# A two-block network on one core: down weights as whole images in the convolutions' buffers, modulation beside the up projection, sums of activations on VectorE alone

## The chip, the core and the metric

The kernel runs on one core of one Trainium2 chip. The metric is the device time of one execution in microseconds (us). The engines of the core work side by side, each through its own list of instructions in a fixed order: TensorE (PE, matmuls, whose weight loads stand as PEld), VectorE (DVE), ScalarE (ACT), GpSimd (POOL), and SyncE (SP), which issues the DMA transfers one behind the other. An instruction waits on semaphores until its inputs are written and its buffer is free, and everything behind it on its engine waits with it.

## The reference

Two blocks run one after the other on 1024 tokens of width 1024. The first has two layers, each an attention mixer and a gated MLP with a short convolution; the second is a recurrent and convolutional mixer whose norms are modulated by a condition vector. What the change touches is the MLP and the two preparations for the second block:

```python
def conv_gated_mlp(h, w_up, conv_w, conv_b, w_down):     # d_ff 2816, so w_up has 5632 columns
    u = h @ w_up
    up = jnp.pad(u, ((0, 0), (half, half), (0, 0)))
    c = conv_b
    for i in range(CONV_W):                               # 3 taps over the tokens
        c = c + up[:, i:i + s] * conv_w[i]
    gate, val = jnp.split(c, 2, axis=-1)
    return (jax.nn.gelu(gate, approximate=True) * val) @ w_down
...
    mod = jax.nn.silu(c) @ mod_w[l] + mod_b[l]            # modulation: 1024 x 3072, two vectors
    mod_k = jax.nn.silu(c_ctx) @ mod_w[l] + mod_b[l]
    hk = rms_norm_2(ctx, norm_g[l]) * (1.0 + scale_k) + shift_k
    vk = jnp.einsum('btd,de->bte', hk, lp['w_in'][:, :BRANCH_W])
    _, state_k = rglru(vk, lp, h0)                        # context: 256 tokens, gives start states
```

All of it is float32. The kernel gets that precision from TensorE by splitting each operand into a rounded high part and a low remainder and adding three products (high by high, high by low, low by high).

## The kernel before

The activations stand with channels on the 128 partitions and tokens along a row, in two halves of 512 tokens (`hf` 0 and 1), so an "image" is one group of 128 output channels for one half of the tokens: a PSUM tile of 128 x 512. Each operand is split by `split` (line 236): a cast on ScalarE (L239) makes the high part, a subtraction on VectorE or GpSimd (L240) the low one. All matmuls of this program part carry line L233.

Buffers come from pools by tag, each with a fixed number of tiles: `wr` (3 tiles of 128 x 512, raw weights as they land), `wh` and `wl` (2 each of 128 x 1024, their split parts), `v` (4 of 128 x 1024, the convolutions' accumulators), `p` (5), `q` (10) of 128 x 1024, `cb` (3 of 128 x 512, copies of PSUM tiles, also used by the context work), `pj`, `pt`, `pf`, `x`. PSUM has the tags `A` (2 tiles of two banks), `T` (2), `O` and `J` (1 each). A scheduler sets the order on each engine from the program's order and the tiles' dependences. So a tile's tag decides whose release a transfer waits for.

`ffn` is one layer's MLP. It runs these stages:

- `up_first` computes the images 0 and 1 of the up projection (the gate and the value half each) directly; `sums` then builds the sums and differences of the activations that the next stage needs.
- `pair(j)` for j = 2 to 21 computes one gate image and one value image for both token halves with seven half-size products (84 matmuls of 512 columns) instead of eight. Weights come in two 512 KB transfers into `q`. The products are joined through copies of PSUM tiles (`kept`, ScalarE, L1075) and additions back into PSUM (`add`, VectorE, L1079); s1 is made on GpSimd, s2 (L1090) and a12 - s2 (L1095) on VectorE, a11 - a21 on GpSimd. Pairs alternate between the PSUM tags T, T, O, J and the two tiles of A. `convolve` (L988 on ScalarE, L993 on VectorE) and `gate` (GELU L1002 on ScalarE, product L1003 on VectorE) finish a pair and store it to `sc_g`.
- `phase(0)`, then `phase(1)`: the down projection for one token half. `down_first(hf)` makes images 0 and 1 and loads the gated activations (`load_g`) on its way; `down(hf, m)` makes images 2 to 7, each in three thirds of 24, 24 and 18 matmuls with 1024, 1024 and 768 weight columns. Every image ends with `put`, a copy out of PSUM on ScalarE (L1159). `finish(0)` (the norm behind the MLP and the next norm) runs inside the start of phase 1, `finish(1)` behind it.

`feed` is work of the second block, given out step by step between the program's own. In layer 0 it is `modulation`, 25 steps: one loads the condition into two `p` tiles, the other 24 each load two chunks of 256 KB (`modw`, L1272) into `wr` and multiply and add them up on VectorE in four operations of 128 x 512 (L1275), each with a read of its sum and a little arithmetic behind. In layer 1 it is `context`, with matmuls of its own and tiles in `cb` and `wr`. `down` takes `n_feed[hf]` steps behind each third: (1, 1) in layer 0, (2, 1) in layer 1.

## Time and profile before

| What | Value |
|---|---|
| median of 3 runs | 3916.99 us (3916.99 to 3918.07) |
| the profiled execution | 3918.27 us, span 3916.5 us |
| TensorE busy | 90% of the span |
| VectorE, ScalarE, GpSimd busy | 63%, 47%, 52% |

"Busy" is the time in which an engine executed something; TensorE can be busy and still run at half the clock, or lose small gaps between matmuls, so the share alone does not tell how far a stage is from its floor. For that one compares a stage's length with its number of matmuls.

| Stage (us from the start of the span) | layer 0 | layer 1 |
|---|---|---|
| `up_first`, `sums`, first pair | 735 to 880 | 2265 to 2400 |
| the other pairs | 880 to 1277 | 2400 to 2806 |
| phase 0, images 2 to 7 | 1277 to 1393 | 2806 to 2950 |
| phase 1, images 0 and 1, with `finish(0)` | 1393 to 1438 | 2950 to 2998 |
| phase 1, images 2 to 7 | 1438 to 1554 | 2998 to 3088 |

### The profile page before, as it was taken

What the parts mean: (1) busy time and instruction counts of PE and PEld (TensorE: products, weight loads), DVE (VectorE), ACT (ScalarE), POOL (GpSimd) and SP (SyncE); (2) the same over time, 40 slices, a digit from 0 to 9 for tenths busy, and PEclk for the clock granted to TensorE, in tenths of its full rate; (3) what the DMA queues carried; (4) which work ended last, traced back from release to release, by engine and by line L of the source; (5) the groups of instructions that cost most, each with busy time, mean ns of one, the idle gap of its engine ahead of it and who ended that gap; (6) DMA issues with size and microseconds to landing.
All of it is one profiled execution on the core that took longest, in us unless ns stands there. A gap on an engine that the chain in (4) does not pass through costs nothing. (4 is left out here: it accounts for less than half of the span.)

```text
span 3916.5 us, 47759 instructions
## 1 busy us (share of the span) xinstructions
PE 3507.2 (90%) x16588; PEld 2833.4 (72%) x16588; DVE 2466.0 (63%) x3384; ACT 1830.7 (47%) x3293; POOL 2028.5 (52%) x1520
## 2 busy tenths in 40 slices
PE   6999899879999878999889888999889989897998
PEld 4788678667777656778778757777767768776786
DVE  5566866776566572467785876656535287686547
ACT  4455755444445232355665544445574323324343
POOL 3445433676557454534543566656656454545444
PEclk9999999899999989999999989999989989998999
DMA  3633653422224453354363432221535211111114
GB/s 98 163 117 124 203 160 124 167 75 76 81 79 137 154 180 127 105 135 152 130 209 129 149 118 81 81 81 64 164 102 165 88 46 55 45 49 38 51 52 142
DMA packets 227841, 440.12 MB, mean 112 GB/s; under 512 B 29584, under 2 KB 56464, under 8 KB 227600
## 3 DMA queue, kind: packets, MB, share of 16 engines
q1 hardware_dynamic: 227600, 437.08, 35.2%
q8 instruction: 130, 2.13, 0.2%
q14 instruction: 111, 0.91, 0.1%
HBM read 313.75 MB, written 104.34 MB: 107 GB/s over the span
## 5 line engine op out<-in xcount | busy, mean ns | idle before, releaser
L240 POOL TENSOR_TENSOR wlZ<-wrZ,whZ 128x512 fp32r<-128x512 f32 (+1 forms) x484 | 665.6, 1391 | 738.1 <-ACT whZ L239 658.3
L233 PE MATMUL AZ<-xZ,whZ 128*128 128x512 f32 x2624 | 830.5, 398 | 75.9 <-ACT cbZ L1075 30.9
L233 PEld LDWEIGHTS AZ<-xZ,whZ 128*128 128x128 f32 x2624 | 497.6, 191 | 198.0 <-ACT cbZ L1075 39.4
L239 ACT CAST whZ<-wrZ 128x512 fp32r<-128x512 f32 (+1 forms) x484 | 277.1, 601 | 633.5 <-issue 163.6
L233 PE MATMUL AZ<-xZ,wlZ 128*128 128x512 f32 x1312 | 522.5, 398 | 19.4 <-POOL wlZ L240 18.8
L524 POOL TENSOR_TENSOR ptZ<-pfZ,ptZ 128x512 fp32r<-128x512 f32 (+1 forms) x200 | 262.6, 1313 | 362.3 <-DVE ptZ L523 330.5
L233 PE MATMUL JZ<-xZ,whZ 128*128 128x512 f32 (+1 forms) x1280 | 415.9, 402 | 35.0 <-DVE xZ L240 7.2
L240 POOL TENSOR_TENSOR wlZ<-qZ,whZ 128x512 fp32r<-128x512 f32 x200 | 264.7, 1340 | 159.6 <-ACT whZ L239 159.6
L522 ACT COPY pfZ<-TZ 128x512 f32<-128x512 f32 (+2 forms) x400 | 220.3, 556 | 206.2 <-PE TZ L517 128.3
L233 PEld LDWEIGHTS AZ<-xZ,wlZ 128*128 128x128 f32 x1312 | 250.8, 191 | 84.2 <-POOL wlZ L240 31.4
L233 PEld LDWEIGHTS JZ<-xZ,whZ 128*128 128x128 f32 (+1 forms) x1280 | 232.2, 187 | 93.6 <-DVE xZ L240 8.3
L233 PE MATMUL TZ<-xZ,whZ 128*128 128x512 f32 x864 | 274.8, 398 | 27.1 <-ACT cbZ L1075 13.2
L540 PE MATMUL OZ<-ptZ,vZ 128*128 128x256 f32 (+1 forms) x1344 | 260.6, 306 | 34.4 <-DVE ptZ L524 11.6
L523 DVE CAST ptZ<-pfZ 128x512 fp32r<-128x512 f32 (+2 forms) x400 | 222.7, 559 | 106.9 <-ACT pfZ L522 91.7
L517 PE MATMUL TZ<-ident,pZ 128*128 128x128 f32 x1488 | 243.4, 283 | 22.0 <-ACT pfZ L522 12.2
L233 PE MATMUL JZ<-xZ,wlZ 128*128 128x512 f32 (+1 forms) x640 | 253.6, 396 | 0.7 <-POOL wlZ L240 0.7
L540 PEld LDWEIGHTS OZ<-ptZ,vZ 128*128 128x128 f32 x1344 | 204.1, 196 | 60.8 <-DVE ptZ L524 17.3
L517 PEld LDWEIGHTS TZ<-ident,pZ 128*128 128x128 f32 x1488 | 181.2, 145 | 54.7 <-ACT pfZ L522 20.9
L239 ACT CAST whZ<-qZ 128x512 fp32r<-128x512 f32 x200 | 116.1, 618 | 213.6 <-issue 139.5
L233 PEld LDWEIGHTS TZ<-xZ,whZ 128*128 128x128 f32 x864 | 164.1, 191 | 68.3 <-ACT cbZ L1075 14.0
L233 PE MATMUL AZ<-qZ,whZ 128*128 128x512 f32 x544 | 179.9, 413 | 26.7 <-ACT pjZ L1159 13.4
L562 DVE TENSOR_REDUCE s1Z<-AZ 128x1 f32<-128x1024 f32 x128 | 155.9, 1221 | 66.2 <-PE AZ L233 35.1
(505 smaller groups left out, 7919.6 us busy)
## 6 DMA issues: line engine op xcount, KB each, us to landing
wrZ<-wdn SPq DMA_DIRECT2D x160, 256.0 KB, 2.8
qZ<-wup SPq DMA_DIRECT2D x80, 512.0 KB, 3.4
wrZ<-wi SPq DMA_DIRECT2D x156, 256.0 KB, 2.7
sc_g<-vZ SPq DMA_DIRECT2D x44, 512.0 KB, 3.4
qZ<-sc_pr SPq DMA_DIRECT2D x40, 512.0 KB, 4.8
wrZ<-wo SPq DMA_DIRECT2D x64, 256.0 KB, 2.9
sc_ot<-cbZ SPq DMA_DIRECT2D x56, 256.0 KB, 2.4
xZ<-sc_ot SPq DMA_DIRECT2D x56, 256.0 KB, 5.6
```

The costliest lines, as they stand in the source:

```text
L233: self.nc.tensor.matmul(ps, lhsT=a, rhs=b, start=first and k == 0, stop=last and k == n - 1, skip_group_check=parts)
L239: nc.scalar.copy(h, full)
L240: (eng or nc.vector).tensor_tensor(out=l, in0=full, in1=h.bitcast(F32), op=ALU.subtract)
L517: nc.tensor.transpose(ps[:, n:n + 128], blk, self.ident)
L522: nc.scalar.copy(pf[:, 0:n], ps[:, 0:n])
L523: nc.vector.tensor_copy(ph[:, 0:n], pf[:, 0:n])
L524: (nc.gpsimd if SHARE[self.turn2 % len(SHARE)] else nc.vector).tensor_tensor(out=pl[:, 0:n], in0=pf[:, 0:n], in1=ph[:, 0:n].bitcast(F32), ...
L540: nc.tensor.matmul(o[:, c0:c0 + w], lhsT=v, rhs=x[:, at[k]:at[k] + w], start=(k == order[0] and x is ph), stop=(k == order[-1] and x is pl ...
L562: nc.vector.tensor_reduce(out=nmx, in_=ps, axis=AX.X, op=ALU.max, negate=True)
```

## The change

Five edits go together.

1. `down` takes its weights through a new `w_tile`: one transfer of the whole third (512 or 384 KB) into a `v` tile, instead of two of 256 KB into `wr`. The split into `wh` and `wl` is still made in pieces of 512 columns, the low part on GpSimd. `down_first` keeps `wr`. `finish(0)` takes its scratch tiles from `cb` instead of `v`.
2. In layer 0 one step of the modulation is given out ahead of each of the 20 pairs; the five that are left go to `phase(0)`. In layer 1 six steps of the context are given out in `down_first(0)`. No steps are left for phase 1.
3. All subtractions and splits of `sums`, and the splits of `prenorm`, are on VectorE. Before, GpSimd had a quarter of the subtractions and half of the splits of `sums`, and every second split of the fast `prenorm`.
4. In `pair` the first copy (p1) goes to a `wr` tile instead of `cb`, and the two PSUM sets are swapped between even and odd pairs. `up_first` uses single banks O, T and J for image 0 and A for image 1, and gates image 1 first.
5. `down_first(0)` uses a tile of A instead of O and T.

```diff
 def finish(hf, pause=None):
-    return nxt(self.post(y[hf], ("ffn_post", l * 8), src, dst, hf, 7 * hf, pause), hf, pause)
+    tag = "v" if hf else "cb"
+    return nxt(self.post(y[hf], ("ffn_post", l * 8), src, dst, hf, 7 * hf, pause, tag), hf, pause, tag)
...
-            def sub(o, x, y, k):
-                (nc.gpsimd if k == 3 else nc.vector).tensor_tensor(out=o, in0=x, in1=y, op=ALU.subtract)
+            def sub(o, x, y):
+                nc.vector.tensor_tensor(out=o, in0=x, in1=y, op=ALU.subtract)
...
-                    self.split(t, h, lo, nc.gpsimd if k % 2 else nc.vector)
+                    self.split(t, h, lo, nc.vector)
...
-            self.split(t, h, l, nc.gpsimd if fast and c % 2 else nc.vector)
+            self.split(t, h, l)
...
-            def kept(ps):
-                t = self.t("cb")
+            def kept(ps, tag="cb"):
+                t = self.raw() if tag == "wr" else self.t(tag)
                 nc.scalar.copy(t, ps)
                 return t
...
-            if j % 2 == 0:
+            if j % 2:
                 c11, c12, c21, c22 = (self.ps(t) for t in "TTOJ")
...
-            p1 = kept(c22)
+            p1 = kept(c22, "wr")
...
-            a = [self.ps("A") for _ in range(2)]
+            a = [[self.ps("O"), None], [self.ps("T"), None]]
...
-            b = [[], []]
-            for v in range(2):
-                b[v].append(self.ps("T" if v else "O"))
-                self.proj(ws[v], xs, 0, b[v][0])
-            for v in range(2):
-                b[v].append(self.ps("T" if v else "J"))
-                self.proj(ws[v], xs, 1, b[v][1])
+            b = [halves(self.ps("A")) for _ in range(2)]
+            for hf in range(2):
+                for v in range(2):
+                    self.proj(ws[v], xs, hf, b[v][hf])
...
             for v in range(2):
+                a[v][1] = self.ps("JT"[v])
                 first(v, 1)
-            gate(0, [convolve(v * 22, [(a[v], 0, T)]) for v in range(2)])
             gate(1, cs)
+            gate(0, [convolve(v * 22, [(a[v][0], 0, 512), (a[v][1], 512, 512)]) for v in range(2)])
...
-            ps = halves(self.ps("A")) if hf else [self.ps("O"), self.ps("T")]
+            ps = halves(self.ps("A"))
...
+                if l and not hf:
+                    feed.step()
                 yield
...
+        def w_tile(src, n):
+
+            raw = self.t("v")
+            nc.sync.dma_start(raw[:, 0:n], src)
+            h, lo = (self.wp.tile([128, 1024], F32R, name=self.nm(t), tag=t, bufs=WB) for t in ("wh", "wl"))
+            for c in range(0, n, 512):
+                c = slice(c, min(n, c + 512))
+                self.split(raw[:, c], h[:, c], lo[:, c], nc.gpsimd)
+            return h, lo
...
-                w = self.weight(I["wdn"][l, m][:, k0 * 128:(k0 + n) * 128], n * 128)
+                w = w_tile(I["wdn"][l, m][:, k0 * 128:(k0 + n) * 128], n * 128)
...
         for j in range(2, 22):
+            if not l:
+                feed.step()
             pair(j, *ts)
-        n_feed = (2, 1) if l else (1, 1)
+        n_feed = (2, 0) if l else (1, 0)
```

Three places show what this does to the engines' lists. On SyncE, in phase 1 of layer 0, before (L208 loads down weights, L1272 the modulation's; the number behind a tag is the tile's):

```order
L1272 DMA wrZ2833_13063<-modw 128x512
L1272 DMA wrZ2836_13069<-modw 128x512
L208 DMA wrZ2841_13079<-wdn 128x512
L208 DMA wrZ2842_13083<-wdn 128x256
L1272 DMA wrZ2843_13105<-modw 128x512
L1272 DMA wrZ2846_13111<-modw 128x512
```

In the changed program SyncE's list has this in the same part of the program, at the end of phase 0 (L1180 is `w_tile`, L1151 is `load_g`):

```order
L1180 DMA vZ2733_12556<-wdn 128x1024
L1180 DMA vZ2736_12588<-wdn 128x768
L1180 DMA vZ2855_13063<-wdn 128x1024
L1180 DMA vZ2858_13095<-wdn 128x1024
L1151 DMA qZ2744_12632<-sc_g 128x512
L1180 DMA vZ2861_13127<-wdn 128x768
L1151 DMA qZ2745_12636<-sc_g 128x512
```

Down weights and modulation no longer alternate in one queue over the same three tiles; the weights of the first third of phase 1 now stand ahead of the loads of the gated activations.

On ScalarE, around the p1 copy of a pair in bank A, before:

```order
L988 ACTIVATE vZ2256_9799<-OZ2241_9668,pv_91 128x512
L239 CAST whZ2266_9868<-pZ2259_9811 128x512
L239 CAST whZ2266_9868<-qZ2257_9809 128x512
L1075 COPY cbZ2264_9835<-AZ2261_9815 128x512
L239 CAST whZ2269_9902<-qZ2258_9810 128x512 x2
L1075 COPY cbZ2265_9865<-AZ2260_9814 128x512
```

In the changed program:

```order
L989 ACTIVATE vZ2231_9441<-OZ2218_9312,pv_91 128x512
L1076 COPY wrZ2245_9491<-AZ2242_9471 128x512
L239 CAST whZ2250_9543<-qZ2238_9465 128x512
L239 CAST whZ2250_9543<-qZ2239_9466 128x512
L239 CAST whZ2253_9577<-qZ2239_9466 128x512
L239 CAST whZ2253_9577<-qZ2263_9625 128x512
L1076 COPY cbZ2248_9523<-AZ2241_9470 128x512
```

The p1 copy now stands ahead of the casts of the next weights; the second copy (p5) stands behind four casts, where it had two.

On VectorE, between a T, T, O, J pair and the next pair in bank A, before (L1003 is the gate's product, L1079 the addition of p1):

```order
L993 SCALAR_TENSOR_TENSOR vZ2218_9507<-OZ2203_9376,pv_91,vZ2218_9507 128x512
L993 SCALAR_TENSOR_TENSOR vZ2218_9507<-OZ2203_9376,pv_91,vZ2218_9507 128x511
L993 SCALAR_TENSOR_TENSOR vZ2218_9507<-JZ2204_9377,pv_91,vZ2218_9507 128x512
L1003 TENSOR_TENSOR vZ2217_9500<-vZ2217_9500,vZ2218_9507 128x1024
L1079 TENSOR_TENSOR AZ2222_9522<-AZ2222_9522,cbZ2226_9543 128x512
```

In the changed program (ISA L1287 are the modulation's operations, L1080 is the addition):

```order
L994 SCALAR_TENSOR_TENSOR vZ2181_9121<-OZ2168_8992,pv_91,vZ2181_9121 128x511
L994 SCALAR_TENSOR_TENSOR vZ2181_9121<-JZ2169_8993,pv_91,vZ2181_9121 128x512
L1287 ISA pZ2208_9293,mpZ2106_8650<-wrZ2207_9291,pZ2085_8500 128x512
L1287 ISA mpZ2106_8650 128x1
L1287 ISA pZ2209_9295,mpZ2106_8650<-wrZ2207_9291,pZ2086_8501 128x512
L1287 ISA mpZ2106_8650 128x1
L1080 TENSOR_TENSOR AZ2191_9150<-AZ2191_9150,wrZ2195_9171 128x512
L1004 TENSOR_TENSOR vZ2180_9114<-vZ2180_9114,vZ2181_9121 128x1024
```

Two of the modulation's four operations stand ahead of the addition of p1, and the gate's product now stands behind it.

## Rows read from the trace of the kernel before

**Rows 1.** Windows: length; busy us (xinstructions) of PE, PEld, DVE, ACT, POOL; PEclk; DMA

```profile
880.00:1277.00 397.00, 372.00 (x1603) 298.21 (x1602) 236.53 (x281) 197.93 (x325) 246.01 (x179) 1.00 0.27 93
1277.00:1393.00 116.00, 98.45 (x399) 73.98 (x398) 71.93 (x184) 33.38 (x59) 47.90 (x39) 0.99 0.56 174
1393.00:1438.00 45.00, 41.21 (x161) 31.67 (x161) 30.41 (x32) 19.48 (x35) 28.83 (x20) 0.92 0.62 196
1438.00:1554.00 116.00, 96.74 (x387) 75.09 (x385) 35.25 (x83) 31.89 (x58) 49.62 (x41) 0.90 0.40 125
2806.00:2950.00 144.00, 120.24 (x541) 96.97 (x539) 58.56 (x83) 97.81 (x171) 75.92 (x66) 0.91 0.39 116
2998.00:3088.00 90.00, 87.18 (x380) 70.88 (x379) 12.00 (x13) 30.46 (x56) 49.35 (x40) 1.00 0.39 117
```

**Rows 2.** Timeline, ScalarE: start, duration, line, operation; copies of the last two images

```profile
1537.65 0.58 ACT L1159 COPY pjZ<-OZ 128x512 f32<-128x512 f32 x1
...
1553.48 0.58 ACT L1159 COPY pjZ<-TZ 128x512 f32<-128x512 f32 x1
```

**Rows 3.** Waits of TensorE, 1277 to 1393: total us, times, longest

```profile
PE AZ L233 <- POOL wlZ L240: 7.3, 12, 1.2
```

**Rows 4.** Waits of TensorE, 1438 to 1554

```profile
PE AZ L233 <- ACT whZ L239: 11.7, 2, 10.1
PE AZ L233 <- ACT pjZ L1159: 5.4, 2, 4.8
```

**Rows 5.** The modulation's line: ns min/median/max, first and last start; its wait

```profile
L1275 DVE CUSTOM_DVE_ANT_0 pZ<-wrZ,pZ x96: 677/689/1769, 1280.0 to 1486.7; 128x512 f32<-128x512 f32 x96
...
  DMA wrZ<-modw: 58.2, 33
```

**Rows 6.** Timeline around 1454; in brackets the idle time before and its releaser

```profile
1453.51 0.62 ACT L239 CAST whZ<-wrZ 128x512 fp32r<-128x512 f32 x1 [6.41 <-DMA wrZ<-wdn]
...
1454.18 1.22 PE L233 MATMUL AZ<-xZ,whZ 128*128 128x512 f32 x2 [10.07 <-ACT whZ L239]
```

**Rows 7.** Waits of TensorE in layer 0's pairs, 880 to 1277

```profile
PE AZ L233 <- ACT cbZ L1075: 19.6, 16, 1.8
PE AZ L233 <- DVE AZ L1079: 2.8, 10, 0.4
```

**Rows 8.** The same in layer 1's pairs, 2400 to 2806

```profile
PE AZ L233 <- ACT cbZ L1075: 19.2, 15, 2.0
```

**Rows 9.** Timeline of one pair of layer 0 in bank A

```profile
1013.76 0.39 PE L233 MATMUL AZ<-xZ,wlZ 128*128 128x512 f32 x1
...
1018.52 0.39 PE L233 MATMUL AZ<-xZ,wlZ 128*128 128x512 f32 x1
...
1020.36 0.72 PE L233 MATMUL AZ<-qZ,whZ 128*128 128x512 f32 x2 [1.46 <-ACT cbZ L1075]
...
1028.19 0.73 PE L233 MATMUL AZ<-xZ,whZ 128*128 128x512 f32 x2 [1.53 <-ACT cbZ L1075]
```

**Rows 10.** Groups of VectorE in layer 0's pairs: busy us, mean ns, idle before

```profile
L993 DVE SCALAR_TENSOR_TENSOR vZ<-AZ,pv,vZ 128x512 f32<-128x512 f32 x37 | 27.7, 748 | 27.9 <-ACT vZ L988 27.6
...
L1079 DVE TENSOR_TENSOR AZ<-AZ,cbZ 128x512 f32<-128x512 f32 x36 | 24.9, 691 | 78.2 <-PE AZ L233 70.1 <-ACT whZ L239 8.1
L1095 DVE TENSOR_TENSOR qZ<-qZ,pZ 128x512 f32<-128x512 f32 x17 | 24.4, 1437 | 0.5 <-POOL wlZ L240 0.4
```

**Rows 11.** DMA issues of the page: KB each, median us to landing

```profile
wrZ<-wdn SPq DMA_DIRECT2D x160, 256.0 KB, 2.8
qZ<-wup SPq DMA_DIRECT2D x80, 512.0 KB, 3.4
```

**Rows 12.** Waits of TensorE, head of layer 0's up projection

```profile
PE TZ L233 <- ACT cbZ L1075: 6.6, 1, 6.6
```

**Rows 13.** Timeline, ScalarE, just before that wait

```profile
832.76 1.06 ACT L1002 ACTIVATE vZ<-vZ 128x1024 f32<-128x1024 f32 x1 [5.46 <-DVE vZ L993]
```

**Rows 14.** Waits of TensorE, layer 1's down projection, 2806 to 2950

```profile
PE TZ L233 <- ACT cbZ L239: 13.6, 3, 8.4
```

More of the change, by code (lines that the diff above doesn't have):

```diff
@@ L290, in mean_sq, with prenorm @@
         return ps
-    def prenorm(self, xn, gain, fast=False, keep=None, pause=None):
+    def prenorm(self, xn, gain, fast=False, keep=None, pause=None, tag="v"):
         nc = self.nc
-        R = self.rstd(self.mean_sq(xn, 1024, fast=fast, bank="T", pause=pause), self.eps, EPS, stay=True)
+        R = self.rstd(self.mean_sq(xn, 1024, tag, fast, "T", pause), self.eps, EPS, tag, stay=True)
         out = []
@@ L329, in load_x, with post @@
         return xn
-    def post(self, y, gain, src, dst, hf, fast=False, pause=None):
+    def post(self, y, gain, src, dst, hf, fast=False, pause=None, tag="v"):
         nc = self.nc
-        R = self.rstd(self.mean_sq(y, 1024, fast=fast, pause=pause), self.eps, EPS, stay=True)
+        R = self.rstd(self.mean_sq(y, 1024, tag, fast, pause=pause), self.eps, EPS, tag, stay=True)
         sl = slice(hf * 512, hf * 512 + 512)
@@ L1036, in sums @@
             for k in range(4):
[L1037 removed]
+                sub(b11[k], b12[k], b11[k])
             put(b11, one("pj"))
             for k in range(4):
[L1040 removed]
+                sub(b12[k], b22[k], b12[k])
             for k in range(4):
[L1042 removed]
+                sub(b22[k], b22[k], b11[k])
             put(b22, lambda k: halves(self.t("q", F32R)))
             for k in range(4):
[L1045 removed]
+                sub(b21[k], b21[k], b22[k])
             put(b12, lambda k: one("pt" if k < 3 else "pf")(k))
@@ L1122, in first @@
             def first(v, hf):
-                ps = a[v][:, hf * 512:hf * 512 + 512]
-                self.mm3(ps, [(tuple(p[:, c % 4 * 128:c % 4 * 128 + 128] for p in own[v][c // 4]), xs[hf][c]) for c in range(8)])
+                self.mm3(a[v][hf], [(tuple(p[:, c % 4 * 128:c % 4 * 128 + 128] for p in own[v][c // 4]), xs[hf][c]) for c in range(8)])
             for v in range(2):
@@ L1285, in modulation, with modnorm @@
                                            op0=ALU.add, op1=ALU.mult)
-    def modnorm(self, xn, which, fast=False, pause=None):
+    def modnorm(self, xn, which, fast=False, pause=None, tag="v"):
         nc = self.nc
-        R = self.rstd(self.mean_sq(xn, 1024, fast=fast, bank="T", pause=pause), self.eps, EPS, stay=True)
+        R = self.rstd(self.mean_sq(xn, 1024, tag, fast, "T", pause), self.eps, EPS, tag, stay=True)
         out = []
@@ L1784, in emit @@
                     feed.add(net.context())
-                    nxt = lambda xn, hf, pause: net.modnorm(xn, 0, fast=hf == 1, pause=pause)
+                    nxt = lambda xn, hf, *a: net.modnorm(xn, 0, hf == 1, *a)
                 xs = net.ffn(l, xs, cur, SC[p], nxt, feed)
```

6 lines of the change are left out of this document (1 added, 5 removed).

## The prediction

> **What bounds the kernel now.** TensorE does, nearly everywhere, so the question for each stage is how much of its time is more than its matmuls need. I first took the spacing of matmuls where nothing stalls: between the two low-part matmuls of [rows 9] at 1013.76 and 1018.52 lie 21 matmuls, so one costs 4.76 / 21 = 0.227 us. Then I read the windows by stage [rows 1] and multiplied the matmul counts by that. Phase 0 of layer 0 (second row): 399 x 0.227 = 91 of 116 us, 25 lost. Phase 1, images 2 to 7 (fourth row): 387 x 0.227 = 88 of 116, 28 lost, with the granted clock at 0.90 of the full 2.4 GHz, so part of the loss is spent in matmuls at the half level of 1.2 GHz. The same stage of layer 1 (last row), which runs beside no fed work: 380 x 0.227 = 86 of 90, 4 lost, clock 1.00. That stage is the control: it uses the old `wr` transfers too, so the loss in layer 0 is not in the down projection itself. Within layer 0 the last image has no modulation beside it, and it took 1553.48 - 1537.65 = 15.8 us [rows 2], where 66 matmuls need 15.0. The pairs of layer 0 (first row of [rows 1]): 1603 x 0.227 = 364 of 397, 33 lost.
>
> Then the waits. In phase 1 of layer 0 TensorE waits 11.7 us for casts of weights in two pieces, and 5.4 us for copies out of PSUM [rows 4]. The longest piece is seen in [rows 6]: TensorE stood 10.07 us for a cast, and ScalarE had itself stood 6.41 us for the transfer of those weights. VectorE stood 58.2 us, in 33 pieces, for the modulation's transfers [rows 5]. Both wait for the other in turn: three `wr` tiles, filled by one queue, hold both kinds, so a weight waits for a reduction and a reduction for a weight's split. In the pairs the waits are short and regular: 16 of about 1.2 us for `kept` copies in layer 0, 15 in layer 1 [rows 7, 8]; [rows 9] show the two of one pair in bank A, for p1 (1.46) and p5 (1.53).
>
> **The change part by part.**
>
> *Layer 0's down projection.* Weights leave `wr`, and 20 of 25 feed steps leave the stage; phase 1 keeps none. If phase 1 then runs like its control it loses 4 / 90 of its length, that is 5 of 116, and gains 28 - 5 = 23. Phase 0 keeps five steps (10 transfers, 20 reductions), in front of a weight queue that they no longer share tiles with; I take 6 lost and a gain of 25 - 6 = 19. The stage between (third row of [rows 1]: 161 x 0.227 = 37 of 45) has the norm inside and stays. Together -42. The upper end is all of both losses, -53; the lower end is what the named waits on weights and copies carry: 11.7 + 5.4 + 7.3 [rows 3, 4] = 24. The 7.3 us for low parts on GpSimd may stay, since `w_tile` splits there too. I take -42, nearer to the control.
>
> Whole images: a third now lands with one 512 KB transfer. By [rows 11] 256 KB took 2.8 us and 512 KB 3.4, so the first half comes 0.6 us later and the second earlier than two in a row; with four `v` tiles the loads stand up to a stage ahead, and I cost this at nothing. Should that lead be lost, it is 0.6 us a third, 18 thirds a phase, 11 us a phase.
>
> *The modulation in layer 0's pairs.* 19 of the 24 groups of reductions move there (the step that loads the condition takes one of the 20 places): four reductions of 0.689 us (median; 0.677 to 1.769, [rows 5]) and about 0.5 of small ones. At the median this is 4 x 0.69 + 0.5 = 3.3 us a pair, at the longest 4 x 1.77 + 0.5 = 7.6. VectorE has 236.5 / 19 = 12.4 us of work in a pair of 397 / 19 = 20.9 us [rows 1], so it goes to 15.7 or, at the worst, 20.0. The reduction's nearest rows are in the same stage: an operation with one operand in SBUF takes 748 ns there, one with two takes 1437 [rows 10]. A reduction has two, so I take 1.44: 4 x 1.44 + 0.5 = 6.3, and 18.7 of 20.9. That fits, but what matters is who is queued behind. In bank A two reductions stand ahead of the addition of p1: 2 x 1.44 + 0.2 = 3.1 us, where the gate's product (about as long as two operations, 1.4 to 2.9) stood before. The next matmuls into that tile come nine matmuls after the p1 product's last, 9 x 0.227 = 2.0 us, and waited 2.8 us in all before [rows 7]. So I add 0.5 us to each of ten such pairs, +5. The other subtractions (s2, a12 - s2) are listed tens of matmuls ahead of their use and are covered. SyncE gets two more transfers a pair behind q2; their tiles come free by reductions of the pair before, so the next q1 waits for no new engine.
>
> The Trainium skill, page "SBUF — State Buffer", section "Who interferes with whom", says that a VectorE instruction with two SBUF inputs and a GpSimd instruction that reads SBUF exclude each other, whichever issued first. The two means in [rows 10] agree with that; by that rule GpSimd is held up as well, and what has to fit into one after the other is GpSimd's 246.0 / 19 = 12.9 us a pair and the reductions' 4 x 0.69, 15.7 of 20.9, so the rule alone does not make the pairs longer.
>
> *p1 in `wr`, ahead of the casts.* On ScalarE the p1 copy no longer stands behind two casts, and the three `cb` tiles serve three copies instead of four. The 1.46 goes; next late is p5, which has four casts ahead of it and two matmuls of fill, 0.45. Half of the 15 waits of [rows 8] are p1's, so layer 1 gains 19.2 / 2 = 10 (nothing if the casts only change places, 17 if most of p5's wait goes too). Layer 0 gains 19.6 / 2 = 10 [rows 7], less 5 for the addition and 3 as an allowance for GpSimd's longer operations: -2 (from -17 to +15).
>
> *The heads.* 16 subtractions and 16 splits for `sums` and every split of the fast norm are on VectorE: 12 of them come new (4 and 8) and 4 in the norm, 16 x 0.68 = 11 us to 16 x 1.77 = 28, by the ends of [rows 5]. VectorE's list there is the chain: the first pair's copy waited 6.6 us [rows 12] behind a GELU that had waited 5.46 for the convolution on VectorE [rows 13]. The new order gates image 1 first and puts the first pair in bank A, so that wait should go; some of what VectorE gained in work comes back elsewhere. I take -5 in each layer, from -14 to +8.
>
> *Layer 1's down projection.* 541 x 0.227 = 123 of 144 us (fifth row of [rows 1]), 21 lost, 13.6 of them in three waits for the context's own chain [rows 14], which stays. Six steps start earlier, and weights and context stop sharing `wr`; against that `finish(0)` now shares `cb` with the context. -4, from -15 to +10.
>
> Sum: -42 - 2 - 10 - 5 - 5 - 4 = -68 on the profiled 3918.3 us, 3850; the median of the runs shown is 1.3 lower, so 3849.
>
> **The rivals.** (1) *Slower: VectorE becomes the bound of layer 0's pairs.* If the reductions run at their longest (20.0 us of work in a pair) and the time for which it stands idle ahead of its additions and of the convolution, 78.2 + 27.9 = 106.1 us [rows 10], cannot be filled, because the list is in order, a pair needs 20.0 + 106.1 / 19 = 25.6 us instead of 20.9: 20 x 4.7 = +94, and with the other terms (-66) +28: 3945. It decides from 3.3 us a pair upward. For it: the 1437 ns. Against: most waits of VectorE in the pairs sit right where a reduction can go. (2) *Half of it in the down stage:* the splits and copies in order bound it, not the tiles; only the 24 us of the named waits go, and layer 0's pairs lose 10: 3849 + 18 + 12 = 3879. It is also the case in which the change does not uncouple what it means to, because `v` loads stand in SyncE's list behind loads of activations that wait for TensorE. (3) *More:* p5's wait goes too in both layers (another 10 + 10), the 8 us set against it in layer 0 don't come, and the heads give 10 each instead of 5: 3849 - 20 - 8 - 10 = 3811.
>
> **How the numbers follow.** Forecast 0.62, (1) 0.08, (2) 0.16, (3) 0.14. The predicted time is the forecast's, 3849. Its terms' ends, taken as independent, give about 30 us to either side; with (2) and (3) inside, the range is 3812 to 3888. A measurement of this kernel can tell about 0.2%, 8 us, from no change. Slower is (1), 0.08, less a little near its threshold, plus a little of (2); same 0.04; faster 0.88.
>
> **What would show it.** Phase 1 of layer 0 at about 93 us with the clock at 1.00, and phase 0 near 97; no TensorE wait over 3 us for a weight's cast there; no p1 wait in bank A, p5 still there; the reductions at a mean near 1.4 us in the pairs, layer 0's pairs within 5 us of 397 and layer 1's near 396; no wait of 6 us at the heads. Wrong if layer 0's pairs pass 450 (then (1)), or if phase 1 of layer 0 stays above 105 with waits for copies or low parts (then (2)).

## The result, and the profile after

The changed kernel takes 3851.28 us (median of 3 runs, 3845.58 to 3852.03); the ratio to the kernel before is 0.9827, with a 95% interval of 0.9805 to 0.9849. The forecast was 3849. Its profiled execution is one of 3845.58 us with a span of 3843.8, so profile against profile the change is -72.7 us. A second measurement beside the experiments gave 3846.09 us and a ratio of 0.9821 (0.9803 to 0.9838).

To see where the time went I compared the two profiles at equal work. Both have 16,588 matmul records, so the n-th matmul of one can be set against the n-th of the other, and the difference of their start times, read at the borders of the stages, tells what each stage gained (a minus is a gain, in us). Near a border a kernel can run its matmuls in another order, so one stage's gain can be the next one's loss. The table gives it for the changed kernel and, to show the spread, for its second profile; for one and the same program the stages differ by up to 2.5 us.

| Stage, by the time in the kernel before | forecast | changed | second profile |
|---|---|---|---|
| 735 to 880, head of the up projection, layer 0 | -5 | +1.3 | +1.2 |
| 880 to 1278, pairs, layer 0 | -2 | +4.7 | +5.9 |
| 1278 to 1393, phase 0, images 2 to 7 | -19 | -20.3 | -20.0 |
| 1393 to 1438, phase 1, images 0 and 1 | 0 | -2.9 | -5.3 |
| 1438 to 1554, phase 1, images 2 to 7 | -23 | -25.4 | -25.5 |
| 2265 to 2400, head, layer 1 | -5 | -0.2 | -0.8 |
| 2400 to 2807, pairs, layer 1 | -10 | -14.2 | -13.7 |
| 2807 to 3088, down projection, layer 1 | -4 | -1.5 | +1.0 |
| everything else | 0 | -14.2 | -15.1 |
| sum | -68 | -72.7 | -72.3 |

The windows of the changed kernel, which answer to [rows 1] (length, busy us and instruction counts of PE, PEld, DVE, ACT and POOL, then TensorE's granted clock, DMA share and GB/s):

```profile
1284.00:1380.00 96.00, 90.66 (x395) 73.47 (x394) 34.05 (x51) 31.62 (x58) 50.90 (x40) 1.00 0.51 166
1380.00:1420.00 40.00, 38.17 (x157) 30.07 (x156) 28.76 (x32) 18.99 (x33) 28.76 (x20) 0.96 0.50 158
1420.00:1509.00 89.00, 85.94 (x376) 69.97 (x374) 10.26 (x12) 29.27 (x56) 48.61 (x40) 1.00 0.31 98
878.00:1262.00 384.00, 357.88 (x1524) 281.82 (x1525) 327.82 (x446) 189.95 (x312) 256.02 (x175) 1.00 0.33 112
2355.00:2718.00 363.00, 351.65 (x1532) 285.48 (x1530) 227.12 (x276) 191.59 (x315) 238.39 (x171) 1.00 0.28 96
2744.00:2885.00 141.00, 117.75 (x538) 96.47 (x537) 48.44 (x72) 86.70 (x152) 75.03 (x67) 0.91 0.40 121
```

The first and third rows are the two image stages of layer 0: 395 matmuls in 96 us and 376 in 89, both at a clock of 1.00, where [rows 1] have 399 and 387 in 116 each, the second at 0.90. At 0.227 us a matmul phase 1 now loses 89 - 376 x 0.227 = 3.6 us: it runs like its control in layer 1. The fourth and fifth rows are the pairs: nearly the same number of matmuls, 384 us in layer 0 and 363 in layer 1. VectorE has 328 us of work in the first and 227 in the second; the modulation's operations stand in the first alone.

TensorE's waits in layer 0's pairs of the changed kernel answer to [rows 7] (total us, times, longest), and GpSimd's in the same stretch follow:

```profile
PE OZ L233 <- ACT whZ L239: 9.9, 8, 1.2
PE JZ L233 <- ACT whZ L239: 9.5, 9, 1.1
PE AZ L233 <- DVE AZ L1080: 3.3, 9, 0.4
```

```profile
POOL wlZ L240 <- ACT whZ L239: 97.9, 41, 3.1
POOL pZ L1087 <- DVE mpZ L1287: 25.0, 8, 3.1
```

The copies that TensorE waited for in bank A [rows 7] are no longer in the list, neither p1's nor p5's, although the prediction expected p5's to stay. In their place stand casts of weights (L239) for J and O; of these, layer 1's pairs have only the wait at J (9.5 us, 9 times). The second fence holds what sets layer 0 apart: GpSimd's s1 (L1087) waits eight times, up to 3.1 us, for the modulation's reductions (L1287) on VectorE. I had seen no link between these two.

### The profile page after: what moved, and what is told of

Its sections match the earlier page's. It is cut to its first block, busy times and chain, and to the rows that moved or that the text cites. A ratio compares the mean times of both kernels' runs of the same rounds, so it can differ in the third digit from the quotient of the medians.

```text
span 3843.8 us, 47537 instructions
## 1 busy us (share of the span) xinstructions
PE 3485.0 (91%) x16588; PEld 2825.7 (74%) x16588; DVE 2513.7 (65%) x3432; ACT 1830.2 (48%) x3300; POOL 1991.0 (52%) x1480
## 5 line engine op out<-in xcount | busy, mean ns | idle before, releaser
L233 PE MATMUL AZ<-xZ,whZ 128*128 128x512 f32 x2880 | 908.7, 397 | 53.3 <-DVE pZ L1571 13.6
L240 POOL TENSOR_TENSOR wlZ<-wrZ,whZ 128x512 fp32r<-128x512 f32 x340 | 488.2, 1451 | 565.6 <-ACT whZ L239 482.9
L233 PEld LDWEIGHTS AZ<-xZ,whZ 128*128 128x128 f32 x2880 | 545.6, 191 | 182.3 <-issue 21.5
L233 PE MATMUL AZ<-xZ,wlZ 128*128 128x512 f32 x1440 | 567.3, 396 | 8.3 <-POOL wlZ L240 7.9
L239 ACT CAST whZ<-wrZ 128x512 fp32r<-128x512 f32 x340 | 196.7, 608 | 417.7 <-issue 140.8
L240 POOL TENSOR_TENSOR wlZ<-qZ,whZ 128x512 fp32r<-128x512 f32 x200 | 279.7, 1413 | 204.5 <-ACT whZ L239 169.5
L233 PEld LDWEIGHTS AZ<-xZ,wlZ 128*128 128x128 f32 x1440 | 274.5, 191 | 71.9 <-POOL wlZ L240 14.1
L517 PE MATMUL TZ<-ident,pZ 128*128 128x128 f32 x1488 | 242.9, 283 | 22.1 <-ACT pfZ L522 12.7
L240 POOL TENSOR_TENSOR wlZ<-vZ,whZ 128x512 fp32r<-128x512 f32 x144 | 181.5, 1280 | 148.4 <-ACT whZ L239 148.1
L233 PE MATMUL TZ<-xZ,whZ 128*128 128x512 f32 x736 | 230.7, 395 | 2.5 <-DVE pZ L256 1.5
L1547 DVE SCALAR_TENSOR_TENSOR vZ<-qZ,pv,vZ 128x1009 f32<-128x1009 f32 (+14 forms) x120 | 193.4, 1630 | 4.1 <-ACT vZ L1537 2.4
```

The lines of the kernel that those rows point to most:

```text
L233: self.nc.tensor.matmul(ps, lhsT=a, rhs=b, start=first and k == 0, stop=last and k == n - 1, skip_group_check=parts)
L239: nc.scalar.copy(h, full)
L240: (eng or nc.vector).tensor_tensor(out=l, in0=full, in1=h.bitcast(F32), op=ALU.subtract)
L517: nc.tensor.transpose(ps[:, n:n + 128], blk, self.ident)
L1547: nc.vector.scalar_tensor_tensor(out=o, in0=i, scalar=w[k], in1=o, op0=ALU.mult, op1=ALU.add)
```

## The experiments

All runs are compared with the kernel before on the same chip, by ratio; the gains by stage come from equal numbers of matmuls, as in the table above.

**Which of the two edits relieved layer 0's down projection?** The first run leaves the modulation where it was, but keeps the weights in the convolutions' buffers, a third of an image in each transfer (the "whole images" of the title are these thirds).

```diff
-            if not l:
-                feed.step()
             pair(j, *ts)
-        n_feed = (2, 0) if l else (1, 0)
+        n_feed = (2, 0) if l else (1, 1)
```

> The changed kernel with one thing undone: the modulation's steps stay beside layer 0's down projection (one behind each third, as before) and none stand beside the pairs; down weights still land in the convolutions' buffers. Theory A (the loss of layer 0's down projection came from weights and modulation sharing three tiles and one queue's order): phases 0 and 1 stay within 10 us of the changed kernel's, the pairs of layer 0 win 10 to 15 back, the total is 3838 to 3850. Rival B (the modulation's own work is what the down projection could not carry): the phases lose 35 to 45 us again, the total is 3875 to 3890.

It took 3841.54 us, ratio 0.9806 (0.9791 to 0.9820), not told apart from the changed kernel. The three down stages gain 10.6, 6.0 and 21.6 us, 38.2 together, against 48.6 in the changed kernel, although all of the modulation stands beside them. VectorE's wait for the modulation's transfers, between 1252 and 1490 us of this run, is:

```profile
DVE pZ L1285 <- DMA wrZ<-modw: 1.2, 2, 0.6
```

In the kernel before it was 58.2 us in 33 pieces [rows 5]. With the weights out of these three tiles next to nothing holds the modulation up. It still costs something there: phase 0 gains 9.7 us less than in the changed kernel. TensorE's largest wait from the start of phase 0's images 2 to 7 to the end of phase 1, first in this run (1252 to 1490), then in the changed kernel (1284 to 1509), is for copies out of PSUM:

```profile
PE AZ L233 <- ACT pjZ L1157: 17.3, 5, 9.0
```

```profile
PE AZ L233 <- ACT pjZ L1157: 7.6, 5, 1.5
```

Layer 0's pairs, now without the modulation, gain 18.3 us, 23 more than in the changed kernel. That is well above the 10 to 15 that I had expected; the run with one output tile below shows why.

The second run is the opposite: the modulation beside the pairs, the weights back in the raw tiles.

```diff
-                w = w_tile(I["wdn"][l, m][:, k0 * 128:(k0 + n) * 128], n * 128)
+                w = self.weight(I["wdn"][l, m][:, k0 * 128:(k0 + n) * 128], n * 128)
```

> The changed kernel with one thing undone: the down weights of images 2 to 7 land in the three raw tiles again, in transfers of 256 KB, while the modulation stays beside the pairs. Theory A (only sharing with the modulation hurt): phase 1 of layer 0, which then has no modulation, stays within 4 us of the changed kernel's; phase 0, where five steps are left, loses 3 to 8; layer 1's first phase, where the context shares the tiles, loses 0 to 6; total 3850 to 3862. Rival W (whole images in deeper buffers are what helps): both phases of layer 0 lose 8 us or more each, total above 3865.

It took 3872.74 us, ratio 0.9869 (0.9845 to 0.9892). Layer 0's stages gain 12.3, 1.7 and 21.8 us: phase 1 loses 3.6 against the changed kernel, phase 0, where five modulation steps are left, 8.0. In layer 1 the stage from 2807 to 2950 is 6.8 us longer than before, 11 more than in the changed kernel. The context's weights share the raw tiles there, and ScalarE's casts wait for the down weights' transfers (2760 to 2910), which is no wait of the changed kernel:

```profile
ACT whZ L239 <- DMA wrZ<-wdn: 12.3, 8, 4.1
```

By 3088 most of that is made up: from 2807 on, this run is 1.3 us longer than the kernel before, 2.8 more than the changed kernel. Either edit alone brings most of layer 0's gain (38.2 and 35.8 of 48.6 us), so most of the loss came from two streams in the same tiles; some 10 us stay lost when the modulation's work stands beside these phases. My expectation, theory A, held for layer 0's two phases, but not for layer 1's first phase (0 to 6 expected) and not for the total, which lies in rival W's range. The rest of the total's difference is spread over stages that the edit does not touch, and no run here explains it.

**Why are layer 0's pairs 19 us longer than layer 1's?** The reductions write products that nobody reads, each into a fresh tile of the pool `p`. Two of its five tiles hold the condition, and s1 takes its tile from the same pool, so s1 must wait until a reduction some places back is done. The next run takes that link away; it is the kernel with one output tile in what follows.

```diff
         cs = [self.t("p") for _ in range(2)]
+        o = self.t("p")[:, 0:512]
...
-                    o = self.t("p")[:, 0:512]
                     nc.vector.tensor_tensor_reduce(out=o, in0=raw, in1=cs[t][:, sl], scale=1.0, scalar=0.0,
```

> The changed kernel with one thing changed: the products that the modulation's reductions write and nobody reads go to one tile held for all of them, instead of a fresh tile from the pool that the pairs' sums on GpSimd (s1) use. Theory P (layer 0's pairs are 19 us longer than layer 1's because GpSimd's s1 waits for a tile that a reduction in VectorE's list must free): GpSimd's wait ahead of s1 goes, casts come earlier, layer 0's pairs win 8 to 15 us, total 3833 to 3842. Rival D (VectorE and GpSimd hold each other up at the operands): less than 3 us, total 3845 to 3852.

It took 3826.05 us, ratio 0.9765 (0.9749 to 0.9782), and in a second run below 3828.69, ratio 0.9768: faster than both kernels. Layer 0's pairs gain 9.5 us where they had lost 4.7. GpSimd's waits there have no row for L1087 any more. TensorE's waits in that stretch, and the reductions (busy us, mean ns) in the changed kernel and then in this one:

```profile
PE JZ L233 <- ACT whZ L239: 10.0, 9, 1.5
PE AZ L233 <- DVE AZ L1080: 5.0, 8, 0.6
```

```profile
L1287 DVE CUSTOM_DVE_ANT_0 pZ<-wrZ,pZ 128x512 f32<-128x512 f32 x66 | 76.6, 1195 | 0.0
```

```profile
L1287 DVE CUSTOM_DVE_ANT_0 pZ<-wrZ,pZ 128x512 f32<-128x512 f32 x68 | 55.2, 812 | 2.4 <-DMA wrZ<-modw 1.2
```

The wait at O is gone together with s1's wait. The reductions are also shorter, 812 ns against 1195, with the same operands: in the changed kernel 34 of the 66 took over 0.9 us, and each of these started while a GpSimd instruction ran; with one output tile it is 8 of 68, and the same holds for them. While s1 waited for a reduction, GpSimd's next work came out right beside the following ones. With the run that has no modulation in the pairs, its price there can be read: without it -18.3, with it and untied -9.5 (-7.4 in the second run), with it and tied +4.7 (5.9 in its second profile). So it costs 9 to 11 us by itself, and the shared tiles cost another 12 to 15. The whole run is 20 us faster than the changed kernel on the same chip; the other 5 to 8 us lie in several stages, and nothing here tells them from spread.

**Do the sums belong on VectorE alone?** This run gives GpSimd its share back (a quarter of the subtractions, half of the splits, every second split of the fast norm).

```diff
-                nc.vector.tensor_tensor(out=o, in0=x, in1=y, op=ALU.subtract)
+            order = iter(range(16))
...
+                k = next(order) % 4
+                (nc.gpsimd if k == 3 else nc.vector).tensor_tensor(out=o, in0=x, in1=y, op=ALU.subtract)
...
-                    self.split(t, h, lo, nc.vector)
+                    self.split(t, h, lo, nc.gpsimd if k % 2 else nc.vector)
...
-            self.split(t, h, l)
+            self.split(t, h, l, nc.gpsimd if fast and c % 2 else nc.vector)
```

> The changed kernel with one thing undone: a quarter of the subtractions and half of the splits of the sums, and every second split of the fast norm, are on GpSimd again. Theory (the heads neither won nor lost by it: 735 to 880 changed by +1, 2265 to 2400 by 0): within 4 us of the changed kernel, either way. Rival (VectorE alone paid for itself, and the new order of the gates lost it again): 5 to 10 us slower at the two heads.

It took 3850.60 us, ratio 0.9831 (0.9813 to 0.9848), not told apart from the changed kernel. The heads moved by +3.7 and -0.7 against the kernel before, where the changed one has +1.3 and -0.2. The windows from 780 to 840 us, of the changed kernel and of this one, tell why:

```profile
780.00:840.00 60.00, 44.38 (x159) 33.00 (x157) 54.80 (x83) 28.80 (x46) 15.96 (x11) 0.86 0.35 119
```

```profile
780.00:840.00 60.00, 41.76 (x155) 31.41 (x154) 53.73 (x62) 27.53 (x44) 41.04 (x26) 0.86 0.32 115
```

VectorE is busy for 54.80 of 60 us with 83 instructions in the one, 53.73 with 62 in the other: what GpSimd takes over, it makes longer on VectorE. One group of splits on VectorE in the same 60 us, in the changed kernel and then in this run, shows it:

```profile
L240 DVE TENSOR_TENSOR xZ<-qZ,xZ 128x512 fp32r<-128x512 f32 x8 | 5.1, 686 | 0.0
```

```profile
L240 DVE TENSOR_TENSOR xZ<-qZ,xZ 128x512 fp32r<-128x512 f32 x4 | 6.9, 1767 | 0.0
```

Half of the splits take longer than all of them did. VectorE's list is full either way.

**What took the copies' waits away in the pairs?** I had put it down to p1's new tile. This run gives p1 its old one.

```diff
-            p1 = kept(c22, "wr")
+            p1 = kept(c22)
```

> The changed kernel with one thing undone: the first copy of each pair (p1) goes to a tile of the three for copies again; the swap of the PSUM sets stays. Theory (the tile is what lets the p1 copy stand ahead of the casts): the p1 waits of 1 to 1.5 us come back in the pairs of one set, layer 1's pairs lose 8 to 15 us, layer 0's as much, total 3862 to 3875. Rival (the swap of the PSUM sets made the gain): within 4 us of the changed kernel.

It took 3862.01 us, ratio 0.9842 (0.9822 to 0.9861). From 2400 to 2750 us, inside layer 1's pairs, the gain is 11.1 us, where the changed kernel has 12.1; one p1 wait of 1.2 us came back. In layer 0's pairs (890 to 1274), where the modulation stands, p1's waits did come back:

```profile
PE AZ L233 <- ACT cbZ L1076: 11.8, 7, 2.0
```

These pairs are not longer for it, though (+3.3 us, against +4.7 and +5.9 in the two profiles of the changed kernel). The larger part of what the total lost was lost in the head of layer 0, +10.8 us instead of +1.3: there TensorE waits once for 7.2 us, for the modulation's operations ahead of the first pair's addition. So the tile serves p1 in layer 0, but my theory fell for the time: it is not what shortened the pairs. The next run leaves p1 its new tile and undoes the swap of the PSUM sets.

```diff
-            if j % 2:
+            if j % 2 == 0:
                 c11, c12, c21, c22 = (self.ps(t) for t in "TTOJ")
```

> The changed kernel with one thing undone: even pairs are on the banks T, T, O, J again and odd pairs on A, as before; p1 keeps its new tile. The run with p1 in its old tile had shown no p1 waits and only 3 us lost in layer 1's pairs, so the tile was not it. Theory S (the swap is what put the p1 copy ahead of the casts in ScalarE's list): the waits of TensorE for copies in bank A come back, 15 to 20 us of them in layer 1's pairs, and these pairs lose 10 to 14 us; total 3862 to 3880. Rival (neither the tile nor the swap alone, but the new up_first): layer 1's pairs lose under 4 us.

It took 3893.56 us, ratio 0.9930 (0.9914 to 0.9947). From 2400 to 2750 us the gain is 1.3 us instead of 12.1. TensorE's waits in this run, first in layer 0's pairs (880 to 1300), then in layer 1's (2380 to 2790):

```profile
PE AZ L233 <- DVE AZ L1080: 26.8, 9, 3.6
PE AZ L233 <- ACT cbZ L1076: 16.5, 9, 4.5
```

```profile
PE AZ L233 <- ACT cbZ L1076: 15.6, 10, 1.8
PE AZ L233 <- DVE AZ L1080: 8.7, 10, 6.3
PE AZ L233 <- ACT wrZ L1076: 3.1, 6, 1.2
```

Since p1 alone is copied to `wr`, the last line is p1's, and the waits for `cb` are those of the other copies. The timeline of one pair of layer 1 shows which: the two waits are the two of [rows 9], p1's first, then p5's.

```profile
2497.92 0.73 PE L233 MATMUL AZ<-qZ,whZ 128*128 128x512 f32 x2 [0.95 <-ACT wrZ L1076]
...
2505.74 0.50 PE L233 MATMUL AZ<-xZ,whZ 128*128 128x512 f32 x1 [1.53 <-ACT cbZ L1076]
```

So what came back without the swap is p5's wait, about 1.5 us in each pair in bank A, in both layers. In the kernel before it had been the larger one already: sorted by the tile that the waiting matmul reads, 13.9 of the 19.2 us of [rows 8] are p5's, in 9 waits, and 5.3 are p1's, in 6. The swap is what took p5's wait away; how it does so, no run here shows.

In layer 0 the p1 addition behind the reductions costs 26.8 us in 9 waits, and layer 0's pairs are 32.6 us longer than in the kernel before; the granted clock over them is 0.96, against 1.00 in the changed kernel, so part of the loss is spent at the lower of TensorE's two levels. This is the wait for the addition that the prediction had priced at +5, on the way to its rival (1), and the swap is what kept it small.

The swap is worth less over the whole of layer 1 than in its pairs. From 2400 to 3088 us, to the end of the down projection, this run gains 12.0 us, the changed kernel 15.7 and 12.7 in its two profiles: up to 2807 this run is 6.9 us longer than before, but the down projection behind is then 18.9 us shorter, where the changed kernel has 1.5.

**Can the last 5 us go, too?** With one output tile TensorE still waited 5.0 us for the p1 addition. This run starts from that kernel and gives two modulation steps ahead of each even pair and none ahead of the odd ones, so that no reduction stands ahead of that addition.

```diff
-            if not l:
+            if not l and not j % 2:
                 feed.step()
+                feed.step()
             pair(j, *ts)
```

> The kernel with one output tile for the reductions, and besides two modulation steps ahead of each even pair and none ahead of the odd ones. In VectorE's list no reduction then stands between a T, T, O, J pair and the p1 addition of the next pair in bank A. Theory (that addition behind two reductions costs what TensorE waits for it, 5.0 us in 8 waits with one output tile): these waits go, layer 0's pairs win 3 to 5 us, total 3820 to 3825. Rival (two steps at once load VectorE's list elsewhere): layer 0's pairs lose 2 us or more.

It took 3872.92 us, ratio 0.9885 (0.9870 to 0.9900): 44 us slower than one step a pair on the same chip, 34 of them in layer 0's pairs, where the granted clock is 0.96 instead of 1.00. The waits for the addition are gone, and a larger one stands in their place:

```profile
PE AZ L233 <- ACT wrZ L1076: 25.9, 8, 3.8
```

The timeline of one of them, on VectorE, ScalarE and TensorE (start, duration, line; in brackets the idle time before and its releaser):

```profile
1001.36 0.69 DVE L1080 TENSOR_TENSOR TZ<-TZ,cbZ 128x512 f32<-128x512 f32 x1
1002.08 0.78 ACT L989 ACTIVATE vZ<-TZ,pv 128x512 f32<-128x512 f32 x1 [5.49 <-DVE TZ L1080]
...
1008.09 0.76 ACT L989 ACTIVATE vZ<-OZ,pv 128x512 f32<-128x512 f32 x1
1008.76 0.57 ACT L1076 COPY wrZ<-AZ 128x512 f32<-128x512 f32 x1
...
1009.38 1.08 PE L233 MATMUL AZ<-qZ,whZ 128*128 128x512 f32 x2 [3.37 <-ACT wrZ L1076]
```

The reductions ahead of it in VectorE's list delay the T addition, ScalarE stands 5.49 us for it with the convolution, and the p1 copy of the next pair is behind that convolution in ScalarE's list. It starts without a gap behind it, so here it waits for the list and not for a tile. To test that against the tile, p1 went back to its old one:

```diff
-            p1 = kept(c22, "wr")
+            p1 = kept(c22)
```

> The kernel with two modulation steps ahead of each even pair, with p1 in its old tile. Theory L (the 25.9 us of waits for the p1 copy there come through the lists: reductions ahead of the T addition on VectorE, ScalarE's convolution waiting for that addition, the p1 copy behind it): layer 0's pairs stay within 6 us of that kernel's, 20 us or more above the kernel with one step a pair. Rival T (five claims on three raw tiles, so the copy waits for a tile that a reduction frees): the waits go and layer 0's pairs win 15 to 25 us.

It took 3861.87 us, ratio 0.9855 (0.9839 to 0.9872); layer 0's pairs lost 5.0 us instead of 26.4. These 21 us are what rival T gave. But the scheduler also spread the reductions differently in this program (some stand between the convolutions of both sets), so the run does not tell the tile from the list, and the question is settled only as far as the timeline above goes.

**Layer 1's down projection.** Two runs start from the kernel with one output tile. One gives the context its old start.

```diff
-                if l and not hf:
-                    feed.step()
                 yield
...
-        n_feed = (2, 0) if l else (1, 0)
+        n_feed = (2, 1) if l else (1, 0)
```

> The kernel with one output tile for the reductions, and besides layer 1's context no longer starts in the first two images of the down projection: two steps behind each third of phase 0 and one in phase 1, as before the change. Theory (the six early steps give layer 1's down projection nothing): layer 1 from the end of its pairs to the end of phase 1 within 5 us of the kernel with one output tile. Rival (they shorten the context's chain, 3 waits of 13.6 us before): 5 to 12 us slower there.

It took 3844.59 us, ratio 0.9798 (0.9778 to 0.9819). From 2807 to 3088 us it loses 6.6 us, where the kernel with one output tile gains 6.0. TensorE's wait for the context's operands is 10.9 us in this run and 1.1 in the kernel with one output tile:

```profile
PE TZ L233 <- ACT cbZ L239: 10.9, 3, 8.9
```

```profile
PE TZ L233 <- ACT cbZ L239: 1.1, 1, 1.1
```

The early steps, with none left for phase 1, are worth 12.6 us to the end of phase 1; I had thought that this chain [rows 14] would stay. In part it did, in another place. In the changed kernel (2744 to 2885), and with one output tile as well, TensorE waits once for a copy out of PSUM:

```profile
PE AZ L233 <- ACT pjZ L1157: 10.4, 1, 10.4
```

The timeline of the changed kernel shows ScalarE and TensorE at its end:

```profile
2846.10 1.28 ACT L175 ACT_TABLE_LOAD   x1
2847.39 0.59 ACT L1157 COPY pjZ<-AZ 128x512 f32<-128x512 f32 x1
...
2848.03 1.22 PE L233 MATMUL AZ<-qZ,whZ 128*128 128x512 f32 x2 [10.38 <-ACT pjZ L1157]
```

The copy stands behind the context's activations in ScalarE's list. Four loads of activation tables, of 1.28 us each, lie in these 10.4 us. To move them was not tried. The other run gives `finish(0)` its scratch tiles from the convolutions' buffers.

```diff
-            tag = "v" if hf else "cb"
+            tag = "v"
```

> The kernel with one output tile for the reductions, and besides the norm behind the first token half takes its scratch tiles from the convolutions' buffers again, beside the down weights. Theory (the weights need all four of these tiles): the starts of phase 1 in both layers lose 2 to 8 us each, total 3830 to 3842. Rival (the lead of the weights is long enough, and the context gets its tiles back in layer 1): the start of phase 1 in layer 1 wins 2 to 6 us, total 3820 to 3826.

It took 3848.13 us, ratio 0.9807 (0.9786 to 0.9828). The starts of phase 1 are 2.4 and 4.9 us longer than in the kernel before, where the kernel with one output tile is 5.4 and 2.9 shorter: about 8 us each (5 to 7 against the second run of that kernel). In layer 1 (2874 to 2928) the longest of TensorE's waits is the norm's own, for an operand that VectorE writes into `v`; the kernel with one output tile has no such wait:

```profile
PE JZ L289 <- DVE vZ L285: 6.3, 1, 6.3
```

That fits norm and weights sharing four tiles; for which tile the operand waits is not shown.

**The spread, and the best kernel again.** The changed kernel was measured a second time, and so was the one with one output tile.

> The changed kernel itself, again, beside the others on the same chip, to tell what is its own spread. Expected 3845 to 3853 us. Theory 'the 8 us gained in layer 1's mixer, whose code is the same, are spread': in this profile the time from the middle of that mixer to its end is within 3 us of the kernel before. Rival 'they come from the order of the lists': the same 6 to 8 us are gained again.

> The kernel with one output tile for the reductions again, on the same chip as the two others, to compare with them. Expected: ratio to the kernel before 0.975 to 0.978, layer 0's pairs 9 to 10 us shorter than in the kernel before.

The second came out with the expected ratio: 3828.69 us, ratio 0.9768 (0.9753 to 0.9782); layer 0's pairs are 7.4 us shorter than before, a little less than the 9 to 10 expected. The first leaves a question open. Between 1930 and 2030 us, in layer 1's mixer, the changed kernel gained 6.5 us, and 5.6 in its second profile, though the change does not touch the code of that stretch. The kernel with one output tile and the one with shared sums, whose code there is the same again, gained -1.0 and 0.6; the run with the modulation in the down projection gained 4.5. So the theory of plain spread did not hold. TensorE's granted clock goes with it in part: over this stretch it is 0.94 in the kernel before, 0.97 in the changed kernel and 1.00 in its second profile, 1.00 in the run with the modulation in the down projection, but 0.97 also in the one with shared sums. Near 3600 to 3680 it is the same with 3.4 us, which the runs either gain or do not: the clock is 0.89 before and 0.91 in the changed kernel. No run here shows why one run has the higher clock there and another has not.

## Why the prediction was right, and where it was not

The total came within 3 us of the median, and that it came so near is luck: the terms that I had planned sum to -58.5 us in the profile instead of -68, and 14 us came from stages that I had left at zero. The largest term was right in mechanism and near in size; of the smaller ones, the pairs and the heads had a wrong mechanism.

*Layer 0's down projection* (forecast -42, measured -48.6). The reading was right in mechanism and near in size: three tiles and one queue for weights and modulation together. The control that I had chosen, phase 1 of layer 1, gave -23 for phase 1 and the measurement -25.4. The two one-sided runs show that either half of the edit would have done most of it, which the prediction did not say. I had left the start of phase 1 at zero; it gained 2.9, and the run with `finish(0)` in the convolutions' buffers shows that the new scratch tiles are part of that.

*Layer 0's pairs* (forecast -2, measured +4.7). The step that failed is "The modulation in layer 0's pairs", which priced the wait on the wrong engine. I priced the p1 addition behind two reductions at +5; in the changed kernel it waited 3.3 us, about as before. What I missed is the tile pool: the reductions' output tiles tie s1 on GpSimd to VectorE's list, 12 to 15 us. On the other hand, the pairs without the modulation gained 18.3 us, where I had set 10 for the copies, so two errors partly cancelled. In the text I had said that the modulation's transfers find their tiles free, and did not ask the same for the tiles that it writes. The duration that I took for a reduction, 1.44 us, was high (mean 1.195): the 1437 ns of [rows 10] are not the price of a second operand alone. All 17 subtractions of that row started while a GpSimd instruction ran; a reduction that meets none takes 0.69 us also in the pairs, and half of them met none. The half microsecond for the small operations was low: in the pairs the addition of 128 x 2 took 1189 ns.

*Rival (1)* did not come. A wait of its kind is real: without the swap of the PSUM sets the addition behind the reductions costs 26.8 us in nine pairs. Layer 0's 20 pairs are then 32.6 us longer, 1.6 us a pair, half of the 3.3 that I gave as the threshold, and the kernel without the swap is still not slower than before. *Rival (3)* has the right sign in one point, p5's wait went too; its time, 3811, lies just outside the range that was to hold it.

*Layer 1's pairs* (forecast -10, measured -14.2). The size was near, the cause was wrong, so the near size is luck. The step that failed is that p1's 1.46 goes, as half of the 19.2 us of [rows 8], and p5's wait is next. P1 had only 5.3 of the 19.2, and p5 had 13.9; both went. I had taken the one pair of [rows 9] for all of them, but p1's wait was over a microsecond in only three of the pairs of either layer. And I had put the gain on p1's new tile, by the order of ScalarE's list; with the old tile 11.1 of 12.1 us stay, without the swap 1.3. The change in that stage had two edits that could set the list, and I ascribed the result to one without a reason to exclude the other.

*The heads* (forecast -5 each, measured +1.3 and -0.2). The step that failed is that the 6.6 us of [rows 12] would go. They did; in the changed kernel other waits for VectorE stand there, the largest two being:

```profile
PE AZ L233 <- DVE AZ L1080: 4.8, 1, 4.8
PE AZ L233 <- DVE vZ L994: 3.9, 1, 3.9
```

I had written that VectorE's list is the chain there and then let a wait go that hangs on it. VectorE was busy for 51.29 of the 60 us from 780 to 840 before and for 54.80 after (5.2 of them the first reductions of the modulation, which I had not counted here); with that the term should have been zero.

*Layer 1's down projection* (forecast -4, measured -1.5): within its bounds. It is the sum of larger numbers that nearly cancel. The early context steps gave 12.6 us and the scratch tiles up to 8; against them stands the wait of 10.4 us for one copy behind the context's activations, where the kernel before has 13.6 us of waits for the context's operands. So the step that failed is that the context's own chain stays as it is: the operands' waits went down to 1.1 us, and most of their length came back at that copy. These figures are from different kernels, and no run adds them up. What edit 5 alone is worth, the bank of `down_first(0)`, was not tried.

## What to carry to other kernels

Ask of work that is moved not only whose queue it joins, but from which pool every tile comes that it reads and writes, results that nobody reads included: a rotating pool ties the engines that take from it, and a held tile for such results cost one line and gave 20 us, 12 to 15 of them in the stage it was meant for. Where two streams share a few buffers, it can be enough to move either the work or the buffers. Where several edits touch the order of one engine's list, the gain cannot be ascribed to one of them from the list alone; undoing one at a time takes a run each. And where waits come in two kinds, sort all of them before taking one pair as typical.

## What the runs showed of the hardware

An addition of 128 x 2 elements took 0.16 us (median) beside the down projection in the kernel before, and a mean of 1.19 us beside the pairs of the changed kernel, where GpSimd works more (256 of 384 us, against 49.6 of 116 [rows 1]):

```profile
1450.74 0.16 DVE L1277 TENSOR_TENSOR mdZ<-mpZ 128x2 f32<-128x2 f32 x1
```

```profile
L1289 DVE TENSOR_TENSOR mdZ<-mpZ 128x2 f32<-128x2 f32 x17 | 20.2, 1189 | 0.3
```

Where the other microsecond goes can be read where GpSimd's and VectorE's rows stand side by side, here twice in layer 0's pairs of the kernel with one output tile:

```profile
1002.80 2.53 POOL L240 TENSOR_TENSOR wlZ<-qZ,whZ 128x512 fp32r<-128x512 f32 x2 [3.16 <-ACT whZ L239]
1002.84 1.27 DVE L1289 TENSOR_TENSOR mdZ<-mpZ 128x2 f32<-128x2 f32 x1
...
1017.18 0.16 DVE L1289 TENSOR_TENSOR mdZ<-mpZ 128x2 f32<-128x2 f32 x1
```

The first of the two starts 0.04 us behind a GpSimd split and takes 1.27 us, the length of one split (two of them in 2.53 us); the second starts while GpSimd does nothing and takes 0.16. All cases are of one or the other kind: of the 58 such additions in the kernel before (24), in the changed kernel's pairs (17) and in the pairs with one output tile (17), 29 took 1.12 to 1.27 us, and each of them started while a GpSimd instruction ran; 29 took 0.15 to 0.16, and none of them did. The profile shows this wait as busy time of VectorE.

The Trainium skill, page "SBUF — State Buffer", section "Who interferes with whom", says that a VectorE instruction with two SBUF inputs and a GpSimd instruction that reads SBUF exclude each other for the whole instruction. The rows agree: the addition has two SBUF inputs, and it ends with the GpSimd instruction (1.27 us against 0.16), whatever its own size. When such work is moved beside GpSimd, its small operations have to be priced like its large ones.
